# Handing plain normalised rows to a mixture of experts, with the first two experts fetched before the ranking

## The chip, the cores and the metric

The kernel runs on one core of a Trainium2 chip. The metric is the device time of one execution in microseconds (us). A core has a matrix engine (PE, TensorE), three elementwise engines (DVE or VectorE, ACT or ScalarE, POOL or GpSimd), a queue engine (SP, SyncE) that here only issues transfers, and 16 DMA engines. Every engine runs its own queue of instructions in order, and waits on semaphores for the others.

## The reference

One layer of a diffusion trunk on 512 tokens of 1024 features, and a mixture of experts behind it. The part around the change, shortened:

```python
mod_l = split(silu(c) @ ada_w + ada_b, 6)          # sh1, sc1, g1, sh2, sc2, g2
...
xl = xl + g1_l * (concat([a_l, b_l, p_l, h_l]) @ w_out)
hl2 = rmsnorm(xl, norm2_g) * (1.0 + sc2_l) + sh2_l
scores = softmax(hl2 @ router_w)                   # 16 experts, 4 groups of 4
# the best group by its two best scores, the two best experts in it,
# gates = their scores over their sum
for e in range(16):
    h = silu(x @ w1[e]) * (x @ w3[e])              # 1024 -> 512
    out = out + gates[:, e:e+1] * (h @ w2[e])      # 512 -> 1024
xl = xl + g2_l * y
return rmsnorm(xl, final_g)
```

Per token the normalised row is scaled by `norm2_g * (1 + sc2)` and shifted by `sh2`, both vectors over the 1024 features.

## The kernel before

**Stages.** The first 420 us compute the modulation, the projections, the attentions, the long convolution and the pooling. Then the last piece of `w_out` and the router run for four tiles of 128 tokens (`wo_unit` L1040, `rlogit` L1109, `rnorm` L1124). A chain of small DVE instructions ranks the tokens of each expert and the experts by their counts (L1176 to L1382). The rest is the mixture: 16 experts of 6 MB each, cut into 6 chunks of 1 MB (chunks 0 to 3 of an expert hold w1 and w3, chunks 4 and 5 w2). The chunks, 96 in all, stream from memory into a ring of 18 slots.

**Router.** For each tile `rlogit` turns the rows (`tH`), copies them to `htr` on ACT and multiplies them with the scaled router weights `rw2`, 16 columns wide, into `plT`. `rnorm` squares the row on ACT, takes the reciprocal root, scales the logits (`lg`, L1134), and makes the rows that the experts read: `hl`, two DVE instructions (L1139) that scale, and two POOL instructions (L1140) that add the shift, for which `sc2b` and `sh2b` are broadcast to all partitions. `hl` goes to the buffer `hld` in memory; the last of these four stores is `put3`.

**Ranking.** `M` (L1216) marks the two experts of each token. Two pairs of matmuls give `pcnt` (counts) and `ppos` (positions). `rk` (L1230) ranks the experts by count. From it come the places of tokens in the table `ids`: `ohp` (L1275), the matmuls `pid` (L1288), `ids` (L1305). `eos` (L1362 to L1366) is the order of the experts; POOL casts it to integers, `eosi` (L1368). `nxi` (L1382) counts experts with more tokens than the table has room for.

**Streaming.** Experts 0 and 1 are always the first two of the flow, so the first ten chunks, counted 0 to 9, have fixed addresses; chunk 10 is the first of an expert by rank, and SP must read that expert's number from `eosi` into a register (L1584). The other 14 experts follow in the order of their counts. The table's first column holds 64 places for expert 0 and 64 for expert 1. At most three loads are in flight (`paced`), and a chunk waits until the chunk 18 before it has been used. The first loads from chunk 9 on also wait behind `put3`. The flag of the overflow branch is read by SP from `nxi` (L1771).

**Experts.** `gather` (L1335) fetches up to 128 rows of `hld` by `ids` into one of two buffers `xg`. `x_prep` (L1408) turns them in 8 transposes `tpx` and evicts them with one ACT and one DVE copy (L1415). `up` (L1450) multiplies into `h`, `act` makes `hs` and its turned form `hx`, `down` (L1517) multiplies into `y`, and `finish` scales by g2 on DVE (`ysb`, L1529) and adds the rows to `xld` in memory by a POOL scatter (L1532). The gates reach `hs` as `gsl` by way of the matmuls `pgt`. At the end `fin` reads `xld` (L1738), and the last expert's rows are added on the chip.

**Order.** A scheduler lays out each engine's queue in program order with priorities; pools of tiles reuse memory, and the SBUF pools wait tile by tile, the PSUM pools as a whole.

Of the kernel before, what the change touches and what calls it, by code (L numbers as in the profile page):

```python
# [20 lines left out]
NE = 16  # L21
# [25 lines left out]
def tile_hybrid_block(ctx, tc, ins, out):  # L47
# [3 lines left out]
    def open_pool(name, side=None, space=None):  # L51
        st = ExitStack()
        kw = {"space": space} if space is not None else {"reuse_waits": "tile"}
# [368 lines left out]
    def ada_fin(i, acc):  # L422
        for q in range(4):
# [627 lines left out]
    def wout1():  # L1051
# [50 lines left out]
    A.copy(b16, p)  # L1102
    rw2 = rt_.tile([128, 8, 16], F32, name="rw2")
    V.tensor_tensor(rw2, rw, mcol[:, 1, :, None].to_broadcast([128, 8, 16]), op=ALU.mult)
    sh2b, sc2b = brow(1, "sh2b"), brow(2, "sc2b")
    V.scalar_tensor_tensor(sc2b, sc2b, 1.0, n2b, op0=ALU.add, op1=ALU.mult)
    plT = {}

    def rlogit(j, half):  # L1109
        p = psb.tile([128, 512], F32, tag="w", name="tH", bufs=4)  # L1110
        for i in range(4):
            k = half * 4 + i
            T.transpose(p[:, i * 128:(i + 1) * 128], xl[j][:, k * 128:(k + 1) * 128], ident)
        ht = we([128, 4, 128], F32, "htr")
        A.copy(ht, p.rearrange("p (c q) -> p c q", q=128))
        if half == 0:
            plT[j] = jbank("plT", (16, 128))
        for i in range(4):
            k = half * 4 + i
            T.matmul(plT[j], rw2[:, k, :], ht[:, i, :], start=(k == 0), stop=(k == 7))  # L1120

    put_h = {}

    def rnorm(j):  # L1124
# [4 lines left out]
        rstd_of(r, r, 1024.0)  # L1129
        lt = we([16, 128], F32, "lt")  # L1130
        A.copy(lt, plT[j])
# [195 lines left out]
    rows_of = lambda col: max(o + r for _, c_, o, r in tiles if c_ == col)  # L1327
    xgs = [mo_.tile([128, 1024], F32, tag="xg", name=f"xg{i}", bufs=NXG) for i in range(NXG)]
    for t in xgs:
        G.memset(t, 0.0)  # L1330

    tab = {"ids": ids}

    def gather(xg, tix, rows=128):
        return G.indirect_dma_start(out=xg[0:rows], out_offset=None, in_=hld[:, :],  # L1335
                                    in_offset=bass.IndirectOffsetOnAxis(ap=tab["ids"][0:rows, 0, tix:tix + 1], axis=0),
                                    bounds_check=511, oob_is_err=False)

    for i in range(NXG):
        gin = gather(xgs[i], cols[i], rows_of(cols[i]))  # L1340
    gate = small([128, 2, 4], "r_gate")
# [12 lines left out]
    V.tensor_sub(vg[:, :, 1], gatef, f(ghi))  # L1354
    pgt = jbank("pgt", (128, 2, NS))
    for k4 in halves:
        lookup(pgt, ohp, oht[1], msk, vg, k4, pid_end, crit)
    gsl = small([128, NS], "r_gsl")
    A.copy(gsl, pgt[:, 0, :])
    gsl_op = V.tensor_add(gsl, gsl, pgt[:, 1, :])  # L1360
    tab["gsl"] = gsl
    behind(V.tensor_tensor(cmp_, rk[:, None, :].to_broadcast([128, 16, 16]),  # L1362
                           iota[:, 0:16, None].to_broadcast([128, 16, 16]), op=ALU.is_equal), crit, False)
    V.tensor_tensor(cmp_, cmp_, iota[:, None, 0:16].to_broadcast([128, 16, 16]), op=ALU.mult)
    eos = small([128, 16], "r_eos")
    V.tensor_reduce(eos, cmp_, axis=AX.X, op=ALU.add)  # L1366
    eosi = small([128, 16], "r_eosi", I32)
    behind(G.tensor_copy(eosi, eos), gin, False)  # L1368
    cap = small([128, 16], "r_cap")
# [17 lines left out]
    NRQ = 5  # L1387
    RQ = [(rc_, "rq", NRQ)] * NRQ
# [19 lines left out]
    def x_prep(xg, get, r=128):  # L1408
        xT = get([128, 8, r], F32, "xT")
        for g in range(2):  # L1410
            p = psm.tile([128, 4, r], F32, tag="tp", name="tpx", bufs=2)
            for i in range(4):
                k = g * 4 + i
                T.transpose(p[:, i, :], xg[0:r, k * 128:(k + 1) * 128], ident[0:r, 0:r])  # L1414
# [164 lines left out]
    def load_w(t, s, c):  # L1579
        if s < 2:  # L1580
            src = mw[s, c]
        else:
            if s not in eids:
                eids[s] = SY.value_load(eosi[0:1, s:s + 1], min_val=0, max_val=NE - 1)  # L1584
            src = mw[bass.ds(eids[s], 1), c].rearrange("e p n -> p (e n)")
# [21 lines left out]
    LP = 9  # L1607

# [84 lines left out]
    for i, (t, c) in enumerate(steps):  # L1693
# [217 lines left out]
def _layout(inp):  # L1911
# [83 lines left out]
```

## Time and profile before

| | us |
|---|---|
| runs of the kernel before | 748.97, 750.80, 753.19 |
| their median | 750.8 |
| the profiled execution | 748.58 |
| its span in the trace | 746.8 |
| PE busy | 652.8 (87%) |
| DVE busy | 369.8 (50%) |
| ACT busy | 245.3 (33%) |
| POOL busy | 148.1 (20%) |

The span is the time between the first and the last instruction of the trace; the execution is 1.8 us longer. Busy shares are averages over stages with different limits. For this change the stretch from 435 us (end of the router) to 465 us (first expert's matmuls) and the expert stage behind it matter; the rows of the trace stand in their own section. In the rows "SPq" is an issue on SP's queue, "<-" in brackets names what ended the idle time before an instruction, and "x" is a count.

### The profile page before, as it was taken

What the parts mean: (1) busy time and instruction counts of PE and PEld (TensorE: products, weight loads), DVE (VectorE), ACT (ScalarE), POOL (GpSimd) and SP (SyncE); (2) the same over time, 40 slices, a digit from 0 to 9 for tenths busy, and PEclk for the clock granted to TensorE, in tenths of its full rate; (3) what the DMA queues carried; (4) which work ended last, traced back from release to release, by engine and by line L of the source; (5) the groups of instructions that cost most, each with busy time, mean ns of one, the idle gap of its engine ahead of it and who ended that gap; (6) DMA issues with size and microseconds to landing.
All of it is one profiled execution on the core that took longest, in us unless ns stands there. A gap on an engine that the chain in (4) does not pass through costs nothing.

```text
span 746.8 us, 10465 instructions
## 1 busy us (share of the span) xinstructions
PE 652.8 (87%) x3984; PEld 417.9 (56%) x3984; DVE 369.8 (50%) x667; ACT 245.3 (33%) x421; POOL 148.1 (20%) x139
## 2 busy tenths in 40 slices
PE   4869999999869999789899964999999899998791
PEld 1457877879857887567788743333444353432230
DVE  3799836777716776993754496111121111211135
ACT  3583313331315675777842241000100010000024
POOL 1127433222205400000000171011111222011122
PEclk9989999999989999968999985999999999999995
DMA  8982357764583572495703564999999999999983
GB/s 316 417 284 96 141 196 259 274 225 146 179 222 109 180 235 79 164 387 230 285 7 140 193 232 154 394 368 391 402 389 392 400 361 382 366 399 409 393 285 116
DMA packets 46353, 197.80 MB, mean 265 GB/s; under 512 B 6297, under 2 KB 13036, under 8 KB 29402
## 3 DMA queue, kind: packets, MB, share of 16 engines
q1 hardware_dynamic: 37466, 173.58, 61.5%
q0 software_dynamic: 7600, 19.68, 8.9%
q10 hardware_dynamic: 1232, 3.82, 1.3%
q8 instruction: 33, 0.54, 0.3%
q14 instruction: 22, 0.18, 0.1%
HBM read 177.66 MB, written 21.12 MB: 266 GB/s over the span
## 4 chain that ended last, share of the span: by engine, by line
PE 54%; DMA 11%; DVE 8%; ACT 4%; issue 2%; SPq 1%; ACTq 0%; DVEq 0%; POOLq 0%
PE h L1450 15%; PE y L1517 6%; DMA mw<-in_moe_w_dram 6%; PE poA L762 3%; DMA xld<-ysb,r_ids 3%; PE pw L75 2%; PE pw L76 2%; PE pw L77 2%; PE y L1503 2%; PE pn L76 2%; PE pn L77 2%; PE pn L75 2%; DMA xld<-ysw,r_ids 1%; DMA kst<-kd 1%; PE pl L75 1%
## 5 line engine op out<-in xcount | busy, mean ns | idle before, releaser
L1450 PE MATMUL h<-mw,xT 128*32 128x256 f32 (+2 forms) x992 | 149.0, 477 | 5.7 <-DMA mw<-in_moe_w_dram 5.6
L1450 PEld LDWEIGHTS h<-mw,xT 128*32 128x32 f32 (+2 forms) x992 | 52.1, 125 | 91.3 <-issue 67.6
L1517 PE MATMUL y<-mw,hx 128*32 128x256 f32 (+2 forms) x464 | 68.1, 470 | 3.5 <-DVE hx L1477 3.0
L1465 ACT ACTIVATE hs<-h 64x512 f32<-64x512 f32 (+2 forms) x22 | 11.1, 506 | 169.3 <-PE h L1450 149.6
L75 PE MATMUL pl<-ht,wh 128*128 128x512 f32 x128 | 52.5, 410 | 3.8 <-DVE bk L72 2.5
L76 PE MATMUL pl<-ht,wh 128*128 128x512 f32 x128 | 51.7, 404 | 0.0
L77 PE MATMUL pl<-ht,wl 128*128 128x512 f32 x128 | 51.5, 403 | 0.0
L1532 POOL DMA_INDIRECT xld<-ysb,r_ids x18 | 28.3, 1570 | 105.8 <-DVE ysb L1529 48.6
L1517 PEld LDWEIGHTS y<-mw,hx 128*32 128x32 f32 (+2 forms) x464 | 24.3, 124 | 38.8 <-issue 27.9
L1466 DVE SCALAR_TENSOR_TENSOR hs<-hs,r_gsl,h 64x512 f32<-64x512 f32 (+1 forms) x13 | 9.7, 743 | 65.8 <-ACT hs L1465 47.5
L72 DVE TENSOR_TENSOR wl<-raw,wh 128x2048 fp32r<-128x2048 f32 x14 | 33.5, 2389 | 13.0 <-ACT wh L71 13.0
L773 DVE TENSOR_REDUCE ml<-s 128x1 f32<-128x768 f32 x32 | 30.3, 950 | 13.5 <-PE s L756 13.1
L774 ACT ACTIVATE eA<-s,ml 128x768 f32<-128x768 f32 x32 | 28.8, 901 | 19.3 <-DVE ml L773 14.6
L71 ACT CAST wh<-raw 128x2048 fp32r<-128x2048 f32 x14 | 26.7, 1908 | 17.6 <-DMA raw<-in_w_in_dram 15.3
L1335 POOL DMA_INDIRECT xg<-hld,r_ids x12 | 12.2, 1017 | 92.9 <-PE tpx L1414 71.2
L75 PEld LDWEIGHTS pl<-ht,wh 128*128 128x128 f32 x128 | 24.4, 191 | 10.2 <-DVE bk L72 2.7
L762 PE MATMUL poA<-aT,av 128*128 128x256 f32 x96 | 26.9, 432 | 1.6 <-DVE aT L802 0.8
L76 PEld LDWEIGHTS pl<-ht,wh 128*128 128x128 f32 x128 | 24.3, 190 | 6.7 <-issue 1.6
L77 PEld LDWEIGHTS pl<-ht,wl 128*128 128x128 f32 x128 | 24.3, 190 | 6.4 <-issue 1.3
L1047 DVE TENSOR_TENSOR xl<-pw,xl 128x512 f32<-128x512 f32 x24 | 16.5, 690 | 22.8 <-PE pw L77 22.6
L1529 DVE TENSOR_TENSOR ysb<-y,g2h 128x512 f32<-128x512 f32 x9 | 6.2, 692 | 41.5 <-PE y L1517 21.1
L75 PE MATMUL pw<-wh,mix 128*128 128x512 f32 x64 | 26.1, 407 | 0.0
(456 smaller groups left out, 1429.3 us busy)
## 6 DMA issues: line engine op xcount, KB each, us to landing
mw<-in_moe_w_dram SPq DMA_DIRECT2D x92, 1024.0 KB
raw<-in_ada_dram SPq DMA_DIRECT2D x24, 1024.0 KB
raw<-in_w_in_dram SPq DMA_DIRECT2D x10, 1024.0 KB
raw<-in_w_out_dram SPq DMA_DIRECT2D x4, 1024.0 KB
mw<-in_moe_w_dram SPq DMA_DIRECT2D x6, 512.0 KB
mixd<-mx SPq DMA_DIRECT2D x5, 512.0 KB
kst<-kd SPq DMA_DIRECT2D x24, 96.0 KB
xin<-in_x_dram SPq DMA_DIRECT2D x4, 512.0 KB
```

Source lines behind the costliest of these rows:

```text
L71: A.copy(hi, src)
L72: (eng or V).tensor_sub(lo, src, f(hi))
L75: T.matmul(ps, a[0], b[0], start=start, stop=False)
L76: T.matmul(ps, a[0], b[1], start=False, stop=False)
L77: T.matmul(ps, a[1], b[0], start=False, stop=stop)
L762: T.matmul(po, avs[:, c, (h // 2) * 128:(h // 2 + 1) * 128], aT[:, c, :], start=(c == 0), stop=(c == 5))
L773: V.tensor_reduce(ml[:, cmp:cmp + 1], s[:, 0:768], axis=AX.X, op=ALU.min)
L774: A.activation(e[:, cmp, :], s[:, 0:768], AF.Exp, scale=-1.0, bias=ml[:, cmp:cmp + 1], accum_out=ml[:, 2 + cmp:3 + cmp])
L1047: V.tensor_add(xv, p, xv)
L1450: T.matmul(p, xk, b, start=(k == 0), stop=(k == 7))
L1517: T.matmul(p, x[k], b, start=(k == 0), stop=(k == 3))
L1532: G.indirect_dma_start(out=dst_, out_offset=bass.IndirectOffsetOnAxis(ap=at_, axis=0), in_=y, in_offset=None, bounds_check=last_, oob_is_e ...
```

## The change

The scale and shift of the second norm no longer happen before the rows are stored. `rnorm` makes plain rows, `x * r`, in one ACT instruction, and stores those. `x_prep` applies scale and shift on the turned rows, where a feature is a partition and both are one number per partition (`mcol`); it takes one instruction per 128 features, 8 instead of 2 per call, four on ACT and four on DVE. The broadcast rows `sh2b`, `sc2b` and `n2b` and their loads are gone (three loads of 512 KB), and the freed memory is one more 1 MB tile of the ring on the router's side, with one fewer opened late (`NRX` 2, `NRQ` 4; the ring still has 18). PSUM pools hand over tile by tile.

`rlogit` pads the router weights to 32 columns and puts its four matmuls of a half into four column groups of the array; `sel16` sums the groups. Copies of odd halves move to DVE.

```diff
-        hl = we([128, 1024], F32, "hl")
-        for n in range(2):
-            cs_ = slice(n * 512, n * 512 + 512)
-            V.scalar_tensor_tensor(hl[:, cs_], xv[:, cs_], r, sc2b[:, cs_], op0=ALU.mult, op1=ALU.mult)
-            G.tensor_add(hl[:, cs_], hl[:, cs_], sh2b[:, cs_])
-        put_h[j] = lambda: A.dma_start(hld[j * 128:(j + 1) * 128, :], hl)
+
+        A.activation(s1, xv, AF.Copy, scale=r)
+        put_h[j] = lambda: A.dma_start(hld[j * 128:(j + 1) * 128, :], s1)
...
-        A.copy(ht, p.rearrange("p (c q) -> p c q", q=128))
+        (V.tensor_copy if half else A.copy)(ht, p.rearrange("p (c q) -> p c q", q=128))
...
-            T.matmul(plT[j], rw2[:, k, :], ht[:, i, :], start=(k == 0), stop=(k == 7))
+            T.matmul(plT[j][i * 32:i * 32 + 32], rw2[:, k, :], ht[:, i, :], start=(half == 0), stop=(half == 1))
...
-        T.transpose(p, lt, ident[0:16, 0:16])
+        T.matmul(p, lt, sel16, start=True, stop=True)
...
+    p01 = small([128, 4, 2], "r_p01")
+    V.scalar_tensor_tensor(p01, pos[:, :, 0:2], 1.0, M[:, :, 0:2], op0=ALU.add, op1=ALU.mult)
+    oh01 = mp([128, 4, 2, 64], F32R, "ohp")
...
+    for j in range(4):
+        T.matmul(pid0, oh01[:, j].rearrange("p a b -> p (a b)"), tk2[:, j], start=(j == 0), stop=(j == 3))
+    ids0 = small([128, 1], "r_ids0", I32)
+    V.tensor_scalar(ids0, pid0[:, 0:1], OOB, None, op0=ALU.add)
+    gather(xgs[0], 0, 128, ids0)
...
+    V.scalar_tensor_tensor(eos[:, 0:16], rk, tokid[:, 0:1], iota[:, 0:16], op0=ALU.is_equal, op1=ALU.mult)
+    A.activation(eos[:, 0:16], eos[:, 0:16], AF.Copy, accum_out=eos[:, 16:17])
+    G.tensor_copy(eosi, eos[:, 16:17])
...
-            (V.tensor_copy if g else A.copy)(xT[:, g * 4:g * 4 + 4, :], p)
...
+                if g and not bank_:
+                    V.tensor_scalar(xT[:, k, :], p[:, i, :], sc, sh, op0=ALU.mult, op1=ALU.add)
+                else:
+                    A.activation(xT[:, k, :], p[:, i, :], AF.Identity, scale=sc, bias=sh)
...
+    xT0, tp0_end = x_prep(xgs[0], mp, 128, jbank)
...
-        ld0 = len(flight)
         load_w(raws[kl], *kl)
-        if LP <= n < NS_:
-            behind(flight[ld0], put3)
...
-    V.tensor_copy(nxi, xi[:, 15:16])
+    behind(V.tensor_copy(nxi, xi[:, 15:16]), rec["yl210"], False)
```

The first two experts' table column is computed as soon as the positions are there (`p01`, `oh01`, `pid0`, `ids0`), and its rows are gathered, turned and evicted (all 8 evictions on ACT) ahead of the gates, whose matmuls `pgt` (`gates()`) move into the loop over the expert steps. `eos` is one DVE and one ACT instruction right behind `rk`. The cast to `nxi` moves to the end of the program, with SP's reading of it.

On SP the order around the first load by number was, with `r_eosi` and `r_nxi` the integers behind `eosi` and `nxi`:

```order
L1587 DMA mw<-in_moe_w_dram 128x2048 x6
L1771 TENSOR_LOAD r_nxi
L1771 ISA x2
L1584 TENSOR_LOAD r_eosi
L1584 ISA x2
```

and is now:

```order
L1605 DMA mw<-in_moe_w_dram 128x2048 x6
L1602 TENSOR_LOAD r_eosi
L1602 ISA x2
L1605 ISA
L1605 DMA mw<-in_moe_w_dram 128x2048
```

The reading of `r_nxi` that stood ahead of the first expert number is now behind the loads of `fin`, at the end of SP's queue.

On DVE, from the counts to the ranks and on (`r_ln`, `r_un`, `r_tb` are the ranking's limits, `p_` its places), before:

```order
L1223 TENSOR_REDUCE r_cnt<-pcnt 128x16
L1249 COPY r_cum<-pcnt 128x16
L1225 SCALAR_TENSOR_TENSOR r_key<-r_cnt,ca 128x16
L1250 TENSOR_TENSOR r_cum<-r_cum,pcnt 128x16
L1253 COPY r_pos<-ppos 128x16
L1227 TENSOR_TENSOR r_cmp<-r_key 128x256
L1251 TENSOR_TENSOR r_cum<-r_cum,pcnt 128x16
L1230 TENSOR_REDUCE r_rk<-r_cmp 128x16
L1254 TENSOR_TENSOR r_pos<-ppos,r_cum 128x48
```

and now:

```order
L1235 COPY r_pos<-ppos 128x16
L1233 TENSOR_TENSOR r_cum<-r_cum,pcnt 128x16
L1251 TENSOR_REDUCE r_cnt<-pcnt 128x16
L1236 TENSOR_TENSOR r_pos<-ppos,r_cum 128x48
L1253 SCALAR_TENSOR_TENSOR r_key<-r_cnt,ca 128x16
L1240 SCALAR_TENSOR_TENSOR r_p_3846<-r_pos,r_M 128x8
L1255 TENSOR_TENSOR r_cmp<-r_key 128x256
L1242 TENSOR_TENSOR ohp<-ca,r_p_3846 128x512
L1258 TENSOR_REDUCE r_rk<-r_cmp 128x16
L1261 SCALAR_TENSOR_TENSOR r_eos<-r_rk,ca 128x16
```

The positions, `p01` (`r_p`) and `oh01` (written as `ohp`) now stand ahead of `rk`, and `eos` right behind it; before, the three instructions of `eos` stood behind both `ohp`.

On PE, from the router's last transposed logits to the experts, before:

```order
L1220 MATMUL ppos<-r_M,ca 128x64
L1288 MATMUL pid<-oht_3905,ohp 128x12 x8
L1288 MATMUL pgt<-oht_3906,ohp 128x24 x8
L1414 MATMUL tpx<-ca,xg_3925 128x128 x8
L1450 MATMUL h<-mw,xT 64x512 x32
```

and now:

```order
L1227 MATMUL ppos<-r_M,ca 128x64
L1246 MATMUL pid_3850<-r_tk_3792,ohp 128x2 x4
L1313 MATMUL pid<-oht_3906,ohp 128x12 x8
L1363 MATMUL tpx<-ca,xg_3794 128x128 x8
L1468 MATMUL h<-mw,xT 64x512 x8
L1313 MATMUL pgt<-oht_3907,ohp 128x24 x8
L1468 MATMUL h<-mw,xT 64x512 x21
```

The four `pid0` matmuls (`pid_3850`) come first, and `pgt` moved from ahead of the first transposes to behind the first eight `h`.

## Rows read from the trace of the kernel before

**Rows 1.** Stretches, core 0: us, busy of each engine, granted clock, DMA share, GB/s

```profile
454.00:456.00 2.00, 0.27 (x2) 0.30 (x2) 1.93 (x10) 0.00 (x0) 0.00 (x0) 0.50 0.00 0
...
458.00:460.00 2.00, 0.83 (x4) 0.83 (x5) 1.35 (x13) 0.00 (x0) 1.09 (x1) 0.50 0.00 0
...
466.00:468.00 2.00, 2.00 (x8) 0.50 (x6) 0.00 (x0) 0.00 (x0) 0.14 (x1) 0.58 0.97 299
...
470.00:710.00 240.00, 226.84 (x1608) 90.43 (x1605) 40.45 (x87) 17.65 (x35) 39.18 (x29) 0.99 1.02 389
```

**Rows 2.** Waits of SP's queue: line, released by: total us, times, longest

```profile
SPq L1587 <- DMA mw<-in_moe_w_dram: 185.8, 79, 4.5
...
SPq L1771 <- DVE r_nxi L1382: 10.6, 1, 10.6
...
SPq L1738 <- DMA xld<-ysb,r_ids: 3.8, 1, 3.8
```

**Rows 3.** Timeline, end of the router: start, us, engine, line, operation, count, idle before

```profile
438.34 1.05 PE L1120 MATMUL plT<-htr,rw 128*16 128x128 f32 x8
...
439.92 3.19 DVE L1139 SCALAR_TENSOR_TENSOR hl<-xl,rs,sc2b 128x512 f32<-128x512 f32 x2
...
441.04 0.23 PE L1133 MATMUL pl<-ca,lt 16*128 16x16 f32 x1 [0.52 <-ACT lt L1131]
...
443.04 0.22 DVE L1134 SCALAR_TENSOR_TENSOR lg<-pl,rs,b 128x16 f32<-128x16 f32 x1
```

**Rows 4.** Timeline, from the counts to the first expert's matmuls

```profile
449.64 0.69 PE L1218 MATMUL pcnt<-r_M,ca 128*128 128x64 f32 x2 [8.38 <-DVE r_M L1216]
...
451.34 0.42 DVE L1230 TENSOR_REDUCE r_rk<-r_cmp 128x16 f32<-128x256 f32 x1
...
454.89 1.29 DVE L1275 TENSOR_TENSOR ohp<-ca,p_r 128x512 fp32r<-128x512 f32 x2
...
457.40 0.42 DVE L1366 TENSOR_REDUCE r_eos<-r_cmp 128x16 f32<-128x256 f32 x1
...
458.82 1.09 POOL L1335 DMA_INDIRECT xg<-hld,r_ids  x1 [11.59 <-DVE r_vg L1354]
...
459.17 1.88 PE L1288 MATMUL pgt<-oht,ohp 128*128 128x24 f32 x8 [1.60 <-DVE oht L1283]
...
461.24 0.20 POOL L1368 CAST r_eosi<-r_eos 128x16 int32<-128x16 f32 x1
...
462.92 1.94 PE L1414 MATMUL tpx<-ca,xg 128*128 128x128 f32 x8 [1.87 <-DMA xg<-hld,r_ids]
...
464.79 5.50 PE L1450 MATMUL h<-mw,xT 128*64 128x512 f32 x18
```

**Rows 5.** Timeline of SP's queue, the first loads by expert number

```profile
462.24 16.08 SPq L1587 DMA_DIRECT2D mw<-in_moe_w_dram  x6
```

**Rows 6.** Chain of waits, last weight loads: start, us, what

```profile
699.81 7.70 DMA mw<-in_moe_w_dram
707.56 1.94 PE h L1450 x8
```

**Rows 7.** Single lines, prices: duration ns min/median/max, first and last start, forms

```profile
L1128 ACT ACTIVATE xsq<-xl x4: 1059/1060/1062, 423.9 to 437.4; 128x1024 f32<-128x1024 f32 x4
...
L1415 ACT COPY xT<-tpx x12: 265/532/586, 464.0 to 666.9; 128x512 f32<-128x512 f32 x6, 128x384 f32<-128x384 f32 x4, 128x256 f32<-128x256 f32 x1, 128x128 f32<-128x128 f32 x1
...
L377 ACT ACTIVATE hc<-xt,md,m x8: 547/560/565, 58.3 to 70.5; 128x256 fp32r<-128x256 f32 x8
```

**Rows 8.** Line 1335, the twelve row gathers, issue to landing

```profile
DMA to landing us min/median/max: 4.0/8.6/9.2
```

**Rows 9.** Lines 1532, 1738: who waits for scatters, `fin` issues; its first use

```profile
  DVE ysb L1529: 44.6, 8
...
L1738 SPq DMA_DIRECT2D fin<-xld x4: 336/403/423, 716.9 to 718.2; - x4
...
726.36 0.67 DVE L1747 TENSOR_TENSOR fin<-pd,fin 128x512 f32<-128x512 f32 x1
```

More of the change, by code (lines that the diff above doesn't have):

```diff
@@ L52, in open_pool @@
         st = ExitStack()
-        kw = {"space": space} if space is not None else {"reuse_waits": "tile"}
+        kw = {"reuse_waits": "tile"}
+        if space is not None:
+            kw["space"] = space
         if side is not None:
@@ L422, in ada_fin @@
     def ada_fin(i, acc):
-        for q in range(4):
+        for q in range(2 * i, 2 * i + 2):
             A.dma_start(rowd[2 * i + q // 2:2 * i + q // 2 + 1, (q % 2) * 512:(q % 2) * 512 + 512],
@@ L1102, in tile_hybrid_block @@
     A.copy(b16, p)
[L1103 to L1106, printed above, removed]
+    rw2 = rt_.tile([128, 8, 32], F32, name="rw2")
+    V.memset(rw2, 0.0)
+    V.tensor_tensor(rw2[:, :, 0:16], rw, mcol[:, 1, :, None].to_broadcast([128, 8, 16]), op=ALU.mult)
+    sel16 = rt_.tile([128, 16], F32, name="sel16")
+    V.tensor_reduce(sel16, ident.rearrange("p (q a) -> p a q", q=4)[:, 0:16], axis=AX.X, op=ALU.add)
     plT = {}
@@ L1114, in rlogit @@
         ht = we([128, 4, 128], F32, "htr")
[L1115 removed]
+        (V.tensor_copy if half else A.copy)(ht, p.rearrange("p (c q) -> p c q", q=128))
         if half == 0:
[L1117 removed]
+            plT[j] = jbank("plT", (128, 128))
         for i in range(4):
             k = half * 4 + i
[L1120 removed]
+            T.matmul(plT[j][i * 32:i * 32 + 32], rw2[:, k, :], ht[:, i, :], start=(half == 0), stop=(half == 1))
     put_h = {}
@@ L1129, in rnorm @@
         rstd_of(r, r, 1024.0)
-        lt = we([16, 128], F32, "lt")
-        A.copy(lt, plT[j])
+        lt = we([128, 128], F32, "lt")
+        (A.copy if j < 3 else V.tensor_copy)(lt, plT[j])
         p = xbank("pl2", (128, 16))
-        T.transpose(p, lt, ident[0:16, 0:16])
+        T.matmul(p, lt, sel16, start=True, stop=True)
         V.scalar_tensor_tensor(lg[:, j, :], p, r, b16, op0=ALU.mult, op1=ALU.add)
         G.dma_start(xld[j * 128:(j + 1) * 128, :], xv)
-        hl = we([128, 1024], F32, "hl")
-        for n in range(2):
-            cs_ = slice(n * 512, n * 512 + 512)
-            V.scalar_tensor_tensor(hl[:, cs_], xv[:, cs_], r, sc2b[:, cs_], op0=ALU.mult, op1=ALU.mult)
-            G.tensor_add(hl[:, cs_], hl[:, cs_], sh2b[:, cs_])
-        put_h[j] = lambda: A.dma_start(hld[j * 128:(j + 1) * 128, :], hl)
+        A.activation(s1, xv, AF.Copy, scale=r)
+        put_h[j] = lambda: A.dma_start(hld[j * 128:(j + 1) * 128, :], s1)
         if j < 3:
@@ L1174, in tile_hybrid_block, with gather @@
     b4 = lambda t: t[:, None, :].to_broadcast([128, 4, 16])
+    tk2 = small([128, 4, 2], "r_tk2", F32R)
+    V.tensor_copy(tk2, ca[:, C_VAL:C_VAL + 4, None].to_broadcast([128, 4, 2]))
+    NXG = 2
+    xgs = [mo_.tile([128, 1024], F32, tag="xg", name=f"xg{i}", bufs=NXG) for i in range(NXG)]
+    for t in xgs:
+        G.memset(t, 0.0)
+    tab = {}
+    def gather(xg, tix, rows=128, ids_=None):
+        at_ = tab["ids"][0:rows, 0, tix:tix + 1] if ids_ is None else ids_[0:rows]
+        return G.indirect_dma_start(out=xg[0:rows], out_offset=None, in_=hld[:, :],
+                                    in_offset=bass.IndirectOffsetOnAxis(ap=at_, axis=0),
+                                    bounds_check=511, oob_is_err=False)
     mx = small([128, 4, 1], "r_mx")
@@ L1221, in tile_hybrid_block @@
     tot = pc_.rearrange("p (j e) -> p j e", j=4)
+    pos = small([128, 4, 16], "r_pos")
+    cum = small([128, 3, 16], "r_cum")
+    V.tensor_copy(cum[:, 0], tot[:, 0])
+    V.tensor_add(cum[:, 1], cum[:, 0], tot[:, 1])
+    V.tensor_add(cum[:, 2], cum[:, 1], tot[:, 2])
+    pp4 = pp_.rearrange("p (j e) -> p j e", j=4)
+    V.tensor_copy(pos[:, 0], pp4[:, 0])
+    V.tensor_add(pos[:, 1:4], pp4[:, 1:4], cum)
+    p01 = small([128, 4, 2], "r_p01")
+    V.scalar_tensor_tensor(p01, pos[:, :, 0:2], 1.0, M[:, :, 0:2], op0=ALU.add, op1=ALU.mult)
+    oh01 = mp([128, 4, 2, 64], F32R, "ohp")
+    V.tensor_tensor(oh01, iota[:, None, None, 1:65].to_broadcast([128, 4, 2, 64]),
+                    p01[:, :, :, None].to_broadcast([128, 4, 2, 64]), op=ALU.is_equal)
+    pid0 = xbank("pid0", (128, 2))
+    for j in range(4):
[3 more added lines that the diff above has]
+    gather(xgs[0], 0, 128, ids0)
     cnt = small([128, 16], "r_cnt")
@@ L1230, in tile_hybrid_block @@
     V.tensor_reduce(rk, cmp_, axis=AX.X, op=ALU.add)
+    eos = small([128, 17], "r_eos")
+    eosi = small([128, 1], "r_eosi", I32)
+    V.scalar_tensor_tensor(eos[:, 0:16], rk, tokid[:, 0:1], iota[:, 0:16], op0=ALU.is_equal, op1=ALU.mult)
+    A.activation(eos[:, 0:16], eos[:, 0:16], AF.Copy, accum_out=eos[:, 16:17])
+    G.tensor_copy(eosi, eos[:, 16:17])
     un = small([128, 16], "r_un")
@@ L1327, in tile_hybrid_block, with x_prep @@
     rows_of = lambda col: max(o + r for _, c_, o, r in tiles if c_ == col)
[L1328 to L1339, printed above, removed]
-        gin = gather(xgs[i], cols[i], rows_of(cols[i]))
+    tab["ids"] = ids
+    for i in range(1, NXG):
+        gin = gather(xgs[i], cols[i], rows_of(cols[i]))
+    def x_prep(xg, get, r=128, bank_=None):
+        xT = get([128, 8, r], F32, "xT")
+        for g in range(2):
+            p = (bank_("tpx", (128, 4, r)) if bank_ else
+                 psm.tile([128, 4, r], F32, tag="tp", name="tpx", bufs=2))
+            for i in range(4):
+                k = g * 4 + i
+                tp = T.transpose(p[:, i, :], xg[0:r, k * 128:(k + 1) * 128], ident[0:r, 0:r])
+            for i in range(4):
+                k = g * 4 + i
+                sc, sh = mcol[:, 1, k:k + 1], mcol[:, 0, k:k + 1]
+                if g and not bank_:
+                    V.tensor_scalar(xT[:, k, :], p[:, i, :], sc, sh, op0=ALU.mult, op1=ALU.add)
+                else:
+                    A.activation(xT[:, k, :], p[:, i, :], AF.Identity, scale=sc, bias=sh)
+        return (xT, tp) if bank_ else xT
+    xT0, tp0_end = x_prep(xgs[0], mp, 128, jbank)
     gate = small([128, 2, 4], "r_gate")
@@ L1354, in tile_hybrid_block, with gates @@
     V.tensor_sub(vg[:, :, 1], gatef, f(ghi))
-    pgt = jbank("pgt", (128, 2, NS))
-    for k4 in halves:
-        lookup(pgt, ohp, oht[1], msk, vg, k4, pid_end, crit)
     gsl = small([128, NS], "r_gsl")
-    A.copy(gsl, pgt[:, 0, :])
-    gsl_op = V.tensor_add(gsl, gsl, pgt[:, 1, :])
     tab["gsl"] = gsl
[L1362 to L1368, printed above, removed]
+    def gates():
+        pgt = psm.tile([128, 2, NS], F32, tag="tp", name="pgt", bufs=2)
+        for k4 in halves:
+            lookup(pgt, ohp, oht[1], msk, vg, k4, None, crit)
+        A.copy(gsl, pgt[:, 0, :])
+        V.tensor_add(gsl, gsl, pgt[:, 1, :])
     cap = small([128, 16], "r_cap")
@@ L1406, in tile_hybrid_block @@
                    put3, False)
[L1408 to L1414, printed above, removed]
-            (V.tensor_copy if g else A.copy)(xT[:, g * 4:g * 4 + 4, :], p)
-        return xT
     fl2 = lambda t: t.rearrange("p a b -> p (a b)")
@@ L1583, in load_w @@
             if s not in eids:
-                eids[s] = SY.value_load(eosi[0:1, s:s + 1], min_val=0, max_val=NE - 1)
+                eids[s] = SY.value_load(eosi[s:s + 1, 0:1], min_val=0, max_val=NE - 1)
             src = mw[bass.ds(eids[s], 1), c].rearrange("e p n -> p (e n)")
@@ L1619, in prep_next @@
         if k < len(cols):
-            xT = x_prep(xgs[k % NXG], mp, rows_of(cols[k]))
+            xT = x_prep(xgs[k % NXG], mp, rows_of(cols[k])) if k else xT0
             for st in sts:
@@ L1700, in tile_hybrid_block @@
             up(st, c, raws[k])
+            if i == 1:
+                gates()
         else:
@@ L1949, in _layout @@
     d["poolw"] = pw
-    d["n2g"] = g["norm2_g"][0]
     d["fg"] = g["final_g"]
```

22 lines of the change are left out of this document (3 added, 19 removed).

## The prediction, made before the changed kernel ran

> **What bounds the kernel now.** I read the stretches first, since the stages have different limits. From 470 to 710 us the DMA engines are full (share 1.02 in the row, 389 GB/s) while PE still has 13.2 us without work, 240 less 226.84; DVE and ACT are busy for 40 and 18 us of it [rows 1]. So the expert stage is bound by the stream of weights. SP's waits say the same: of all its waits the largest by far is a weight load that waits for an earlier one, 185.8 us in 79 times [rows 2], which is the limit of three in flight. The end of the chain of waits closes the argument: the last weight loads, then the last matmuls that wait for them [rows 6]. From there on the work to the end is fixed. The time therefore follows the moment at which the stream starts and what it must carry, as long as nothing else becomes late.
>
> The stream starts late. From 454 to 460 us the DMA engines move nothing [rows 1]: the fixed loads are done, and the first load by expert number goes out at 462.24 [rows 5]. What it waits for is read backwards [rows 4]: the cast `eosi` at 461.24 stands on POOL behind two gathers (`xg`, from 458.82), these wait for `ids` behind `ohp` and `pid`, and `eos`, done at 457.8, stands on DVE behind `ohp`. `rk`, all that `eos` really needs, was ready at 451.34 + 0.42 = 451.76. SP also reads `nxi` first, 10.6 us in that wait [rows 2], but `nxi` is there at about 459.3, earlier than `eosi`.
>
> **The router's end.** `lg` of the last tile runs at 443.04, though its input `pl` ended at 441.27: DVE was in two `hl` instructions from 439.92 to 443.11 [rows 3]. Without these `lg` could follow at about 441.45, a gain of 1.6. The column groups can also shorten `plT`, 1.05 us for four matmuls [rows 3]; four at once would take at least 0.26, so for the last two groups of four the gain is between 0 and 1.6. Against it, ACT now makes the plain rows: priced by the square over the same 1024 columns, 1.06 each [rows 7], and one of them stands ahead of the last tile's square. The ends are 1.6 - 1.06 = 0.5 and 1.6 + 1.6 = 3.2. I take **2.5**, near the upper end, since PE is the engine that the last tile waits for, and the copies on DVE relieve ACT by 0.58 each.
>
> The row shows 1.05 us for a group of four, and nothing before shows one that is switched between shapes of the array in this way. The Trainium skill (TensorEngine Tiling (Array Packing), section Key Properties) states that a change of tiling mode drains TensorE, and each group here stands between full-width transposes; by it the column groups would buy little, where its table in section Theoretical Speedup promises up to four times. By the first the shift is near 0.5 and not 2.5. No run shows which yet.
>
> **The first expert number.** After the counts DVE has more to do ahead of `rk`: the positions, `p01`, and `oh01`, half of the 1.29 us of the two `ohp` [rows 4], with the rest about 0.85. `rk` ends at 451.76 + 0.85 = 452.6. Then `eos` on DVE, a sum on ACT, the cast on POOL: 0.2 (the cast's row) on POOL, and I allow 0.6 for the two before, between 0.4 and 1.0, because three engines hand over. From the cast's start to the load it took 462.24 - 461.24 = 1.0 before [rows 4, 5]; `nxi` is no longer ahead of it. Together 452.6 + 0.6 + 1.0 = 454.2, less 2.5: the load goes out at 451.7 instead of 462.24, **10.5 us earlier**. With the shift at 0.5 it is 8.5, with 3.2 it is 11.2.
>
> Not all of it reaches the stream. Two gathers of 128 rows of 4 KB, 1.05 MB, at 389 GB/s [rows 1] are 2.7 us of all engines. Before, the first ran mostly ahead of the stream, and now both lie inside; the part that is new is between 0 and 2.7, and I take 1.3. The stream gains **9.2**, between 7.8 and 10.5 with the shift at 2.5. The dropped loads of 1.5 MB lie before 440 us and buy nothing at the end.
>
> **The first expert's rows and PE.** `ids0` needs `oh01`, four short matmuls and one DVE step. With `oh01` done at about 452 and some 1.5 us to the gather's issue, less 2.5, this is about 451. The first gather of before took 4.0 us to land, the smallest of the twelve, with the engines idle; the median, under full load, is 8.6 [rows 8]. It now meets the stream's first loads, so I take 5.0 with ends 4.0 and 8.6. Transposes 1.94 [rows 4] and the last eviction follow: 451 + 5.0 + 1.9 + 0.7 = 458.6 for the first `h`, where it was 464.79, 6.2 earlier; `pgt` with 1.88 us [rows 4] moves behind it, so PE's work gains **4.3**, between 0.7 and 5.3. This is less than the stream gains. PE can make it good: it has the 13.2 idle us, and needs 9.2 - 4.3 = 4.9 of them. The clock matters too: 0.50 granted until PE has worked for a while, 0.58 at 466 to 468 [rows 1], and an earlier start moves that slow stretch forward without making it longer.
>
> The scatters into `xld` are the second thing that follows PE. They run one behind the other, DVE's `ysb` waits for them 44.6 us in 8 times [rows 9], and the loads of `fin` wait for the last one, 3.8 us [rows 2], going out at 716.9. The first use of `fin` is at 726.36 [rows 9]. A load of 512 KB that takes some 4 us leaves about 4.2 of slack. So this chain allows 4.3 + 4.2 = **8.5** before it is late next. The lesser of 9.2 and 8.5 less a little for both being close: **8.0**.
>
> **Other edits.** Each `x_prep` has eight small evictions. ACT's with scale and shift took 0.56 for 256 columns and a plain copy of 128 columns 0.265 at least [rows 7], so 128 columns cost about 0.45 by an estimate from both; four are 1.8 against 0.585 of one copy of 512. That is 1.2 more for ACT per call, and about 0.9 for DVE by the same reasoning, for eleven calls after the first; ACT's 13.4 us lie beside PE and the stream, on an engine that is busy for 18 of 240 us. I cost it at nothing; the cover is PE's work of other tiles, already queued between `x_prep` and its use. Tile-wise PSUM pools, the ring's other split and the last fixed load without its wait: between -0.5 and +0.5, taken as 0. The late `nxi` costs SP one register read while DVE prepares the end.
>
> The sum against the profiled execution: 748.58 - 8.0 = 740.6. The median of the runs is 2.2 longer than that execution, 750.8, and so the forecast there is **742.8**.
>
> **The rivals.**
> - *PE or the scatters bound.* The gather lands in 8.6 us, PE gains 0.7 to 2, the scatters then allow 0.7 + 4.2 = 4.9, with ends to 6.2: 750.8 - 5.5 = 745.3. For it: the gather meets a full stream. Against: its issue lies at or ahead of the first load's.
> - *Column groups buy nothing.* Shift 0.5 instead of 2.5, everything 2 earlier is lost: 8.0 - 2.0 = 6.0, 744.8. Against: no row either way. The Trainium skill's drain, above, is this case.
> - *More than that.* The gathers cost nothing, shift 3.2, and the scatters have more slack: 11.2, 739.6.
> - *Nothing moves.* The first load is out early, but PE and the ring of 18 slots set the pace again, or the stream's mean speed falls with it: 750. Against: PE's 13.2 idle us.
> - *Slower: the evictions.* ACT carries 1.2 us more per call in a queue with the `hs` activations, and DVE behind `ysb`, which itself waits for scatters [rows 9]. If each call's eviction is late for its tile's `h` on PE, up to 11 x 1.2 = 13.4 land on PE, plus 11 x 0.9 of DVE: 750.8 - 8 + 13.4 = 756.2. It decides from an exposure of 8 us on, and is slower by 0.5% (754.6) from 11.8. Against: each `x_prep` is queued a tile ahead of its use. The Trainium skill (TensorEngine Tiling (Array Packing), section PSUM Bottleneck) warns that the copy out of PSUM may become the bottleneck behind a faster TensorE, which is this case's kind.
>
> **How the numbers follow.** Forecast, 740.3 to 744.3: 0.47. PE or scatters, 744.3 to 747: 0.18. Column groups: 0.06. More, below 740.3: 0.13. Nothing, to 754: 0.10. Slower: 0.06. About 0.5%, 3.75 us, is what a measurement of this kernel can tell from no change, so faster means below 747.05: 0.47 + 0.18 + 0.06 + 0.13 = 0.84; same 0.10, slower 0.06. The range from 737.0 to 748.0 holds the first three, most of the fourth and a part of the fifth, 0.84 in all: 0.71 + 0.11 + 0.02.
>
> **What would show it.** Right: the first load by expert number at about 452 instead of 462, with no DMA gap of 6 us; `lg` of the last tile near 440.5; first `h` near 458.6; last weight load 8 to 9 us earlier; SP's wait on `nxi` gone. Wrong: `plT` still 1.05 per group of four; a gather that lands after 8 us; weight loads that wait for PE's use of a slot; idle PE in front of `h` that waits for `xT`; a `fin` whose first use waits for its load.

## The result and the profile after

The changed kernel takes 740.65 us (median of 4 runs, 739.1 to 741.73), the kernel before in the same comparison 749.88. The ratio is 0.9872, with a 95% interval from 0.9837 to 0.9907; on the 750.8 us of the forecast that is 741.2 (738.6 to 743.8). The forecast was 742.8. A second comparison of the same kernel, over five rounds, gave 0.9861 (0.9823 to 0.9899). The profiled run has a span of 737.1 us, 9.7 less than before.

These stretches of the changed kernel have the columns of [rows 1]: us, busy time of PE, its weight loads, DVE, ACT and POOL, granted clock, DMA share, GB/s.

```profile
444.00:446.00 2.00, 1.12 (x4) 0.93 (x4) 1.14 (x9) 0.00 (x0) 0.44 (x1) 0.50 0.06 21
446.00:448.00 2.00, 0.78 (x4) 0.81 (x4) 1.97 (x12) 0.29 (x2) 0.00 (x0) 0.50 0.00 0
448.00:450.00 2.00, 0.20 (x1) 0.11 (x1) 1.84 (x12) 0.01 (x1) 0.95 (x2) 0.50 0.00 0
450.00:452.00 2.00, 0.11 (x1) 0.14 (x1) 1.95 (x9) 0.00 (x0) 0.42 (x1) 0.50 0.82 238
...
456.00:458.00 2.00, 0.00 (x0) 0.00 (x0) 0.00 (x0) 0.00 (x0) 0.00 (x0) 0.50 1.00 412
...
530.00:540.00 10.00, 10.00 (x58) 3.40 (x49) 1.97 (x4) 1.35 (x3) 1.59 (x1) 1.00 0.81 309
...
460.00:700.00 240.00, 232.30 (x1631) 92.20 (x1631) 48.37 (x123) 30.93 (x76) 39.89 (x29) 0.99 1.01 382
```

The gap without transfers, from 454 to 460 in [rows 1], has not gone: it now lies from about 445 to 450, 5 us instead of 6, because the fixed loads are also done earlier. At 456, in the middle of the old gap, the share is 1.00. PE's time without work in 240 us of the expert stage fell from 13.2 to 7.7. New is the row at 530: the DMA engines, full in the ten us on either side of it and at this place in the kernel before, drop to 0.81 while PE is busy for all ten us.

The same places as in [rows 3] and [rows 4], on the changed kernel's timeline:

```profile
422.08 0.29 PE L1096 MATMUL b<-rsum,ca 128*128 128x16 f32 x2
...
434.78 0.43 PE L1116 MATMUL plT<-htr,rw 128*32 128x128 f32 x8
...
436.55 0.23 DVE L1130 SCALAR_TENSOR_TENSOR lg<-pl,rs,b 128x16 f32<-128x16 f32 x1
...
444.26 0.69 PE L1225 MATMUL pcnt<-r_M,ca 128*128 128x64 f32 x2 [8.25 <-DVE r_M L1223]
...
446.99 0.41 DVE L1258 TENSOR_REDUCE r_rk<-r_cmp 128x16 f32<-128x256 f32 x1
...
448.08 0.19 POOL L1263 CAST r_eosi<-r_eos 128x1 int32<-128x1 f32 x1 [3.64 <-ACT r_eos L1262]
...
449.25 1.17 POOL L1178 DMA_INDIRECT xg<-hld,r_ids  x1 [0.97 <-DVE p_s L1286]
449.37 24.45 SPq L1605 DMA_DIRECT2D mw<-in_moe_w_dram  x10
...
458.05 1.97 PE L1363 MATMUL tpx<-ca,xg 128*128 128x128 f32 x8 [4.32 <-DMA xg<-hld,r_ids]
...
459.95 4.57 PE L1468 MATMUL h<-mw,xT 128*64 128x512 f32 x16
...
464.45 1.06 PE L1313 MATMUL pgt<-oht,ohp 128*128 128x24 f32 x8
```

The work before the router ends at another time in every execution, between 419.7 and 424.2 us over the traces of this study. So all readings below are taken from the start of the matmul of the router's offsets (`b`, the first row here; in the trace of before this row stands at 422.63). Four of the `plT` matmuls of the source are eight instructions in the trace, x8 in the row. The first load by number then came at 27.3 and not at 39.6, the first `h` at 37.9 and not at 42.2.

SP's waits in the changed kernel, behind 447 us (line, released by: total, times, longest):

```profile
SPq L1605 <- DMA mw<-in_moe_w_dram: 176.7, 74, 4.3
SPq L1602 <- POOL r_eosi L1263: 15.8, 1, 15.8
SPq L1605 <- PE y L1535: 12.2, 5, 5.3
SPq L1753 <- DMA xld<-ysb,r_ids: 7.8, 1, 7.8
```

The third row is the new one: a weight load waits for PE to have used the slot, 12.2 us, where before it was 0.8. The wait on `nxi` [rows 2] is gone; SP now waits 15.8 us for the first expert number itself, so this number still decides when the stream starts. The last row answers to the 3.8 us of [rows 2]: the loads of `fin` still wait for the last scatter.

### The profile page after: what moved, and what is told of

Read it like the earlier page. It is cut to its first block, busy times and chain, and to the rows that moved or that the text cites. A ratio compares the mean times of both kernels' runs of the same rounds, so it can differ in the third digit from the quotient of the medians.

```text
span 737.1 us, 10538 instructions
## 1 busy us (share of the span) xinstructions
PE 652.6 (89%) x3992; PEld 416.2 (56%) x3992; DVE 369.5 (50%) x699; ACT 260.1 (35%) x462; POOL 135.5 (18%) x129
## 4 chain that ended last, share of the span: by engine, by line
PE 53%; DMA 8%; DVE 7%; ACT 4%; issue 2%; SPq 0%; ACTq 0%; DVEq 0%
PE h L1468 19%; PE y L1535 7%; DMA mw<-in_moe_w_dram 3%; PE poA L764 3%; PE pw L77 2%; PE pw L78 2%; PE pw L79 2%; PE y L1521 2%; PE tpx L1363 2%; DMA kst<-kd 2%; DMA xg<-hld,r_ids 1%; DVE wl L74 1%; PE tB L995 1%; PE tph L1493 1%; PE poB L1008 1%
## 5 line engine op out<-in xcount | busy, mean ns | idle before, releaser
L1468 PE MATMUL h<-mw,xT 128*32 128x256 f32 (+2 forms) x992 | 151.2, 480 | 4.8 <-DMA mw<-in_moe_w_dram 4.2
L1535 PE MATMUL y<-mw,hx 128*32 128x256 f32 (+2 forms) x464 | 66.5, 465 | 0.0
L1370 ACT ACTIVATE xT<-tpx,mcol 128x128 f32<-128x128 f32 (+3 forms) x52 | 18.5, 440 | 53.6 <-PE tpx L1363 53.5
L764 PE MATMUL poA<-aT,av 128*128 128x256 f32 x96 | 28.6, 456 | 1.1 <-ACT aT L804 0.8
L1048 DVE TENSOR_TENSOR xl<-pw,xl 128x512 f32<-128x512 f32 x24 | 16.5, 691 | 23.2 <-PE pw L79 23.0
L1178 POOL DMA_INDIRECT xg<-hld,r_ids x12 | 12.3, 1026 | 84.8 <-PE tpx L1363 75.2
L1368 DVE TENSOR_SCALAR xT<-tpx,mcol 128x128 f32<-128x128 f32 (+3 forms) x44 | 13.8, 376 | 27.0 <-PE tpx L1363 27.0
## 6 DMA issues: line engine op xcount, KB each, us to landing
xin<-in_x_dram SPq DMA_DIRECT2D x4, 512.0 KB, 11.7
```

Of the source, the lines that this page charges most:

```text
L764: T.matmul(po, avs[:, c, (h // 2) * 128:(h // 2 + 1) * 128], aT[:, c, :], start=(c == 0), stop=(c == 5))
L1370: A.activation(xT[:, k, :], p[:, i, :], AF.Identity, scale=sc, bias=sh)
L1468: T.matmul(p, xk, b, start=(k == 0), stop=(k == 7))
L1535: T.matmul(p, x[k], b, start=(k == 0), stop=(k == 3))
```

## The experiments

All numbers but the ratio are us; the times from `lg` to "last y" are starts in the profiled run, less the start of `b`. "load" is the first load by expert number, "last y" the first sixteen `y` matmuls of the last expert (709.32 before, 700.38 after), "slot waits" SP's waits for PE's `y`, the third row above.

| kernel | lg | pcnt | load | first h | last y | slot waits | ratio to before (95%) |
|---|---|---|---|---|---|---|---|
| before | 20.4 | 27.0 | 39.6 | 42.2 | 286.7 | 0.8 | 1 |
| changed | 14.5 | 22.2 | 27.3 | 37.9 | 278.3 | 12.2 | 0.9872 (0.9837 to 0.9907) |
| e1_plain16 | 18.5 | 25.3 | 30.4 | 41.1 | 284.9 | 14.0 | 0.9922 (0.9893 to 0.9951) |
| e2_groups_alone | 18.3 | 27.7 | 40.3 | 43.1 | 288.5 | 0.3 | 1.0022 (0.9988 to 1.0057) |
| e3_psum_whole | 14.5 | 22.2 | 27.3 | 40.0 | 282.7 | 16.0 | 0.9933 (0.9902 to 0.9965) |
| e4_two_evictions | 14.5 | 22.2 | 27.3 | 38.0 | 277.6 | 10.8 | 0.9889 (0.9854 to 0.9925) |
| e5_eos_alone | 20.4 | 27.0 | 31.1 | 46.8 | 290.0 | 15.2 | 0.9982 (0.9949 to 1.0016) |
| e6_eos_late | 14.5 | 23.2 | 39.0 | 35.7 | 289.4 | 1.6 | 0.9964 (0.9936 to 0.9991) |
| e7_gather_late | 14.5 | 22.3 | 27.0 | 42.4 | 284.0 | 21.0 | 0.9968 (0.9933 to 1.0003) |
| e8_load11_behind_gather | 14.5 | 22.0 | 27.1 | 34.9 | 278.2 | 2.4 | 0.9875 (0.9815 to 0.9936) |
| e9_same | 14.5 | 22.9 | 28.0 | 38.6 | 278.9 | 11.9 | 0.9861 (0.9823 to 0.9899) |
| e10_load12_behind_gather | 14.5 | 22.8 | 27.9 | 38.2 | 279.2 | 9.3 | 0.9884 (0.9844 to 0.9923) |

The starts up to the counts agree to about 0.1 between kernels with the same router, but for 0.6 to 1.0 at `pcnt` in three of them. A ratio's interval is some 2.5 us to either side (4.6 in e8). Against both measurements of the changed kernel together, a difference under some 3 us is not told apart. The other columns are one execution each: that of e6 was 3.7 us longer than its kernel's median, that of e2 3.7 shorter, all others lie within 2.5.

Theory A says that PE was what the router's end waited for. Theory B says that the expert stage now has two limits of nearly the same height, the start of the stream and PE's first `h`, tied together by the ring of slots; its rivals say that one of the two alone counts.

**e1: the column groups taken back.**

```diff
-            T.matmul(plT[j][i * 32:i * 32 + 32], rw2[:, k, :], ht[:, i, :], start=(half == 0), stop=(half == 1))
+            T.matmul(plT[j], rw2[:, k, :], ht[:, i, :], start=(k == 0), stop=(k == 7))
...
-        T.matmul(p, lt, sel16, start=True, stop=True)
+        T.transpose(p, lt, ident[0:16, 0:16])
```

> The changed kernel with the four router matmuls of a half in one group of 16 columns again, accumulating into one plT, and the sum by sel16 taken out; all else stays. Theory A (PE was what the whole router end waited for, and the column groups shortened it): plT is back at 1.05 us per four instead of 0.42, lg of the last tile comes 3 to 5 us later than 436.55, the first load by expert number and the end as much later, so 3 to 5 us over the changed kernel. Rival (the hl instructions on DVE were it, and the groups shorten only what other engines hide): lg at most 1 us later, time within 1 us of the changed kernel.

Four `plT` matmuls again take what [rows 3] shows, on this kernel's timeline:

```profile
420.05 0.29 PE L1096 MATMUL b<-rsum,ca 128*128 128x16 f32 x2
...
436.82 1.05 PE L1113 MATMUL plT<-htr,rw 128*16 128x128 f32 x8
...
438.51 0.23 DVE L1127 SCALAR_TENSOR_TENSOR lg<-pl,rs,b 128x16 f32<-128x16 f32 x1 [0.32 <-PE pl L1126]
```

`lg` comes 4.0 later, the counts 3.1 and the first load 3.1; the ratio is 0.0050 higher than the first and 0.0061 than the second measurement of the changed kernel, some 4 us. Theory A holds: 8 groups, each 0.62 to 0.63 us longer, are 5.0 us, of which 4.0 reach `lg`. What is left of the gain in `lg`, 20.4 - 18.5 = 1.9, is the rest of the edit (`hl` off DVE and copies moved to it); it was not run by itself.

**e2: the column groups alone, in the kernel before.** Its diff is that of e1 the other way round, on before, with the widened `rw2` and `sel16`.

> The kernel before with the column groups and the sum by sel16 alone; hl stays on DVE and POOL. Theory A with hl as the next bound: plT 0.42 per four, but DVE's two hl per tile, 2.4 us each tile under contention with POOL, take PE's place; lg 1 to 3 us earlier than 443.04 and the time 1 to 3 us shorter. Rival 1 (PE alone sets it): lg 4 to 6 us earlier, time 4 to 6 us shorter. Rival 2 (a drain between shapes eats the gain): plT near 1 us per four and no change of the time.

DVE's timeline behind the last `lg`:

```profile
438.73 0.23 DVE L1137 SCALAR_TENSOR_TENSOR lg<-pl,rs,b 128x16 f32<-128x16 f32 x1 [0.46 <-DVE rs L215]
438.88 2.66 DVE L1142 SCALAR_TENSOR_TENSOR hl<-xl,rs,sc2b 128x512 f32<-128x512 f32 x2
441.47 0.20 DVE L1179 TENSOR_REDUCE r_mx<-lg 128x4 f32<-128x64 f32 x1
```

`lg` is 2.1 earlier, and the counts 0.7 later than before: `hl` now stands behind `lg` and keeps the ranking's first step waiting. Theory A had `lg` right, but all three theories missed the place of that wait, and the time did not move measurably. The groups bring their 3 us only where `hl` has left DVE. The other way round this is not so: with `hl` off DVE and no groups (e1) the counts are still 1.7 earlier than before.

**e3: PSUM pools handed over as a whole.**

```diff
-        kw = {"reuse_waits": "tile"}
-        if space is not None:
-            kw["space"] = space
+        kw = {"space": space} if space is not None else {"reuse_waits": "tile"}
```

> The changed kernel with the PSUM pools handed over as a whole again. Theory: nothing of the gain hangs on it, time within 1 us of the changed kernel. Rival: the early turning of the first rows needs a bank that was just read, and a wait for whole pools holds the first h by 2 us or more; then the time is 1 to 3 us longer.

```profile
464.17 5.11 PE L1466 MATMUL h<-mw,xT 128*64 128x512 f32 x16 [2.14 <-ACT xT L1368]
```

This row of its timeline shows the rival at work: the first `h` waits 2.14 us for ACT's evictions of the turned rows, whose bank is in the pool that must be free as a whole, and starts 2.1 later after `b`. The ratio is 0.006 to 0.007 higher, 4.6 to 5.4 us, more than either theory gave and more than the 2.1, though the intervals just touch. Why it is more than the delay wasn't settled.

**e4: two plain copies per `x_prep`.** The eight small evictions became two plain copies, of up to 512 columns; scale and shift are left out.

> The changed kernel with two plain copies per x_prep instead of eight small evictions; the scale and shift of the second norm are left out of the experts' rows, so that only the time is read. Theory (ACT and DVE have room beside PE): time within 1 us of the changed kernel, the first h up to 1 us earlier. Rival (the small evictions are exposed): 3 to 8 us shorter.

The first `h`, the last `y` and the ratio are those of the changed kernel within their spread. The small evictions cost busy time (all `xT` evictions together take ACT 18.5 us and DVE 13.8 in the changed kernel, 6.7 and 6.4 in e4) and no time at the end that can be measured.

**e5: the early expert numbers alone, in the kernel before.** `eos`, `eosi` and `nxi` as in the change, nothing else.

> The kernel before with the early expert numbers alone: eos by one DVE and one ACT instruction right behind rk, the cast ahead of the gathers, and nxi at the end. The first load by expert number goes out at about 454 instead of 462.24. Theory (the ring: PE starts no earlier, its first gather lands later under the full stream, and the stream soon waits for slots that PE has not freed): h starts 2 to 4 us later than 464.79, SP's waits on PE rise by over 5 us, and the time falls by no more than 3 us or rises. Rival (the stream's start is what counts): 7 to 8 us shorter.

The wait of the first transposes, and SP's wait for slots:

```profile
464.62 1.94 PE L1411 MATMUL tpx<-ca,xg 128*128 128x128 f32 x8 [7.01 <-DMA xg<-hld,r_ids]
```

```profile
SPq L1584 <- PE y L1514: 15.2, 5, 9.2
```

The load is 8.5 earlier, and the time doesn't change measurably. The gather, behind three loads of 1 MB, holds the first `h` back by 4.6, and SP then waits 15.2 us in all for slots of the ring. The rival "stream alone" would have the kernel 7 to 8 us shorter; it is out.

**e6: the changed kernel with the expert numbers late again.**

```diff
-    G.tensor_copy(eosi, eos[:, 16:17])
...
+    behind(G.tensor_copy(eosi, eos[:, 16:17]), gin, False)
```

> The changed kernel with the cast of the expert numbers behind the second gather on POOL, as before the change. The first load by expert number goes out at about 457 instead of 449.4, the first gather lands alone in 4 to 5 us and h starts at about 455.5 instead of 459.95. Theory (both limits are near each other): the stream loses 7.5 but no longer waits for slots, some 3 us of this come back, so 3 to 5 us over the changed kernel. Rival 1 (stream alone): 7 to 8 us longer. Rival 2 (PE's start alone): 3 to 4 us shorter.

```profile
451.45 1.18 POOL L1178 DMA_INDIRECT xg<-hld,r_ids  x1 [5.72 <-DVE p_s L1285]
...
455.58 1.97 PE L1363 MATMUL tpx<-ca,xg 128*128 128x128 f32 x8 [5.17 <-DMA xg<-hld,r_ids]
...
462.34 10.20 SPq L1605 DMA_DIRECT2D mw<-in_moe_w_dram  x4
```

The cast went further back than I had expected, so the load lost 11.7 and not 7.5. The gather lands in 4.1 us when it has the engines to itself, the first `h` is the earliest but one of all (2.2 later than I expected, since `pid` now stands ahead of it on PE), and still the kernel loses 7 to 8 us against the changed one. So PE's start alone isn't it either. The loss is more than the theory's 3 to 5 and the same number as that of the rival "stream alone", but for a load that is later by 11.7 this rival would lose as much as that.

**e7: the first gather behind the ranking again.** `p01`, `oh01`, `pid0` and `ids0` are out.

> The changed kernel without the early table column: p01, oh01, pid0 and ids0 are out, and the first gather goes by ids like the others. rk and the first load by number come about 0.7 us earlier, the first gather goes out at about 453 and h starts at about 464. Theory (both limits): 3 to 4 us over the changed kernel, with more waits of SP for slots. Rival (stream alone): within 1 us of it, or shorter.

```profile
SPq L1594 <- PE y L1524: 21.0, 7, 9.0
```

The load stays early and the first `h` is 4.5 later; the slot waits grow to 21.0 us, and the time by 7 to 8, again more than the delay and twice what the theory gave (3 to 4). The rival "stream alone" (no loss) is out. Without the early gather the early stream is worth little, 0.9968 beside 1.

**e8 and e10: the first gather given room.** One wait in each: the second (e8, `n == 11`) or third (e10, `n == 12`) load by number waits for the first gather.

```diff
-    gather(xgs[0], 0, 128, ids0)
+    g0 = gather(xgs[0], 0, 128, ids0)
...
+        ld0 = len(flight)
         load_w(raws[kl], *kl)
+        if n == 11:
+            behind(flight[ld0], g0)
```

> The changed kernel with one wait added: the second load by expert number (chunk 11) and what is behind it on SP go out only when the first gather has landed, so that the gather shares the DMA engines with one load and not three. Theory (both limits): the gather lands after 5 to 7 us instead of 8.8, h starts 2 to 3 us earlier, the stream loses about 1 us in its first loads and loses less at slots: 1 to 2 us shorter than the changed kernel. Rival (stream alone): 1 us longer.

Stretches of e8, columns as above, and its waits for slots:

```profile
454.00:456.00 2.00, 1.17 (x6) 1.08 (x6) 1.81 (x18) 0.00 (x0) 0.00 (x0) 0.50 0.84 344
456.00:458.00 2.00, 1.37 (x7) 1.37 (x8) 0.22 (x2) 0.22 (x1) 1.02 (x1) 0.50 0.41 63
458.00:460.00 2.00, 2.00 (x7) 0.72 (x7) 0.00 (x0) 2.00 (x7) 0.99 (x1) 0.50 0.80 324
530.00:540.00 10.00, 10.00 (x50) 3.58 (x47) 1.97 (x4) 1.34 (x3) 1.59 (x1) 1.00 1.02 395
```

```profile
SPq L1605 <- PE y L1535: 2.4, 3, 1.7
```

The first `h` starts 3.0 earlier, the dip at 530 is gone and the slot waits nearly so, as the theory has it. But the engines are at 0.41 from 456 to 458 where the changed kernel is full, and the last `y` comes at the same moment: what PE gained the stream lost in its first loads. e9 is the changed kernel beside e10.

> The changed kernel itself, unchanged, on the same chip and in the same rounds as the next run, for the comparison. Every theory: about 0.987 of the kernel before; relative to the end of the router the same times as in its first profile (first load by number 27.3 us after the matmul of the router's offsets, first h 37.9 us after it).

> The changed kernel with the third load by expert number (chunk 12), and what follows on SP, behind the landing of the first gather, so that two loads and not one run beside it. Theory (both limits are near each other; in the run with chunk 11 held back the DMA engines fell idle and the stream lost what PE gained): no idle DMA before 460, the gather lands in 7 to 8 us, h starts 1 to 2 us earlier than in the changed kernel, SP's waits on PE fall below 12 by some us, and the time is 0.5 to 2 us shorter than the changed kernel. Rival (the end has another limit by now, the scatters into xld): no change.

With two loads beside it the gather still took 8.5 us from issue to the first transpose (449.79 to 458.31), and nothing was won: 0.9884 beside 0.9861, intervals overlapping. Neither beats the changed kernel, as far as these intervals can tell.

Taken back one at a time, four edits cost about 4 (e1), 5 (e3), 7 (e6) and 7.5 us (e7), over twice the whole gain of about 10. So they need one another at least in part, and the gain can't be split into one share for each. The ring's other split, the last fixed load without its wait and the late `nxi` were not run alone, nor was a ring with more slots.

## Why the prediction was right, and where its steps were not

The time fell inside the range and near the forecast, by the mechanism named: the stream starts earlier, PE starts earlier by less, and PE makes the rest good out of its idle time. The last `y` came 8.4 us earlier and the end, by the ratio, 9.6, where 8.0 was forecast. Taken one by one the terms were worse than their sum, and that it came out so close is in part luck.

- **The router's end: mis-sized.** I took 2.5 between 0.5 and 3.2. The counts came 4.8 earlier, `lg` 5.9. The step that failed is "for the last two groups of four": at the measured 0.42 two groups give 1.3, and e1 prices all eight at 4.0 of the 5.9. A drain that eats the gain, as the Trainium skill names it (TensorEngine Tiling (Array Packing), section Key Properties), doesn't show: four matmuls took 0.42 and not 1.05 us between full-width transposes, 2.5 times as fast, below the up to four times of that page's table.
- **The first expert number: right.** From the counts to the load 5.1 now, 12.6 before: 7.5 of the 8.0 that I worked out. `rk` came 1.0 later behind the counts (0.85 expected), and from its end to the load it took 2.0 (1.6). With the larger shift the load was 12.3 earlier and not 10.5.
- **The first gather: outside its ends.** It took 8.8 us to the first transpose, where I took 5.0 between 4.0 and 8.6. The value to take was the median under load, and not one near the smallest; e6 and e8 measure 4.1 and 5.9 (450.69 to 456.63) with no and one load beside it. So the first `h` gained 4.3 and not 6.2, in spite of a router that was 2.3 better. With `pgt` behind it (1.06) PE's work gained 3.2, where 4.3 was forecast; with some 5 us of idle time made good that is about the 8.4 at the last `y`. The bytes were wrong as well: in e6, where the gather runs alone, 0.32 MB moved, 77 rows of 4 KB, and not the 0.52 MB of 128. By the 389 GB/s of [rows 1] I estimate these at 0.8 us; what the rest of the 4.1 is was not settled.
- **The stream's gain, 9.2: the ring was left out.** I charged it with the gathers only. It gained 12.3 at its start, and SP then waited 12.2 us for slots that PE freed too late, where before it was 0.8. Not all of this is lost, since other loads are in flight: the last weight load goes out 8.6 earlier (701.2 and 710.3, less `b`), within the 8 to 9 of the forecast. The slot waits were one of my signs for "wrong", and they are what makes PE's start count as much as the stream's. That an early start better than forecast and a ring left out came to the forecast again is luck.
- **The scatters: nearer, but not the limit.** The loads of `fin` went out 5.7 earlier (711.2), their first use 9.0 earlier (717.40): the time between went from 9.4 to 6.2. It is still enough: that first use, an addition on DVE, starts 0.05 after the end of the two `pd` matmuls ahead of it, as in the trace of before, and from the last `y` to the end it takes 36.7 us now and 37.5 before. The profile does name the load of `fin` for the idle time of POOL's first instruction on `fin`; but this starts 0.14 after DVE's addition in both traces, so no loss is shown.
- **The small evictions at nothing: right** (e4). ACT's evictions take 18.5 us where they took 6.1, so 12.5 more, near the 13.4 priced, without a trace at the end.
- **The gap of the DMA engines: a sign that did not come.** I named "no DMA gap of 6 us" as a sign of being right; there is still one of about 5, before the first load by number. The fixed loads were done some 9 us earlier too, with the last of them freed from its wait, an edit that I took at nothing and that was not run alone.
- **PSUM pools at nothing: wrong.** I gave ±0.5 and named no cover. e3 makes it 4.6 to 5.4 us. The early turning of the first rows uses a bank of the router's pool, and only a hand-over tile by tile lets the first `h` start behind the first eviction.

In the table this reads as one rule, good to 1 or 2 us: where the load is early (27 to 31), the last `y` follows the first `h`, from 278.3 and 37.9 (changed) over 282.7 and 40.0, 284.9 and 41.1 (e1), 284.0 and 42.4 to 290.0 and 46.8; where the load is late, an early `h` is worth little (e6, 0.9964). In e8 `h` is earlier than 37.9 and `y` the same, but there the second load is later too, so whether PE's start alone would still help the changed kernel is not shown.

## What to carry to other kernels

When a stream through a ring starts earlier, its consumer must start earlier too, or the ring hands part of the gain back; look for slot waits far behind the start (here at 530 to 560, 80 us and more), not at it. A small transfer that the consumer waits for shares the engines with the stream that is started beside it: price it by the row under load. An edit that frees one engine may be worth nothing until the next engine on the same step is freed (e2), so cost such edits together.

## What the runs showed of the hardware

A gather of up to 128 rows of 4 KB, 0.32 MB in e6, took 4.1 us from issue to the first use when alone (e6), 5.9 beside one load of 1 MB (e8), and 8.5 to 8.9 beside two (e10) or three (changed, e4, e9). Four matmuls of 128 x 32 weights in four column groups took 0.42 us where four of 128 x 16 weights in one group took 1.05, at the same 128 columns. The work ahead of the router, the same in all, ended 4.5 us apart over these twelve traces, so that differences of a stage are to be read from a row inside it.
